# Attention scores over a ring of key tiles: one wide product per head in place of four narrow ones, and a 128-row low operand

## The chip, the cores and the metric

The kernel runs on one core of a Trainium2 chip. The core has five engines that run on their own and meet at semaphores: PE (matrix products; a product has a stationary operand that a separate load, PEld, brings in, and a moving operand that streams past it), DVE (vector), ACT (scalar functions), POOL, and SP, which here only issues transfers. The metric is the device time of one execution in microseconds (us). The kernel before takes 3162.19 us, the median of 3 runs from 3161.32 to 3166.99.

## The reference, cut to what matters

The program computes two blocks of a network on a sequence of 2048 positions. The change touches one part of the second block, an attention over a band of keys with 4 heads of width 64:

```python
q = rms_norm(q, q_g); k = rms_norm(k, k_g)
# a chunk of 64 queries sees its own chunk of keys and the 8 chunks before it
s = jnp.einsum('bqhd,bkhd->bhqk', qb, kb, preferred_element_type=jnp.float32) * scale + bias
p = jax.nn.softmax(s, axis=-1)
out = jnp.einsum('bhqk,bkhd->bqhd', p, vb)
```

Beside it the block has a linear recurrence over chunks (the names m_...), a convolution branch (c_...), two gates (the dense products called oz below) and an output product (fo).

## The kernel before, in words

The sequence is cut into 16 tiles of 128 positions. `cores` runs a loop over i = 0 to 15. Pass i finishes the attention of tile i (softmax weights turned by transposes, `a_turn`, tile pt; the product with the values, `a_pv`, tile pv) and already makes the scores of tile i+1: `a_own(i + 1)` the scores of the 4 heads against the tile's own 128 keys (tile s5 in the listings, s in the trace), `a_old(i + 1, h)` those of head h against up to four older key tiles (tile s4, also s in the trace). Tile 1 has one older tile, tile 2 two, tile 3 three, tiles 4 to 15 four.

Keys are held as two float16 numbers, a high and a low part. `kring` is a ring of 8 key tiles: partitions 0 to 63 hold the high part of the 64 key dimensions, partitions 64 to 127 the low part, then ring place, head, 128 keys. The query operand `qa` has the high part of q twice, in partitions 0 to 63 and 64 to 127, so that one product gives q-high times k-high plus q-high times k-low. The operand `ql` has the low part of q in 64 partitions, and meets the high part of the keys alone. A head's scores against one key tile are thus two products of 128 columns that add up in PSUM, one of 128 rows and one of 64 (`scored`, lines 1557 to 1562).

The order on every engine is the order of the calls in the loop, written out by hand. Between the attention and recurrence steps, `fill` puts in parts of a queue of dense products: one part is 3 products of 512 columns (oz, line 1465; from pass 14 on also fo, line 1839). `weave` puts in small DVE steps. All steps take their PSUM from four banks "b"; a bank is given out again when its last reader in program order is done. From pass 14 on each `fill` also carries one step that prepares the output weights (wo, lines 1825 and 1826: one ACT and one DVE instruction), from a tile wf that `stage` loads.

On DVE, `lowest` (line 1579) takes scores and bias and leaves the negative sum and its row minimum; on ACT, `a_soft` (line 1599) takes the exponential. For the turned weights ACT writes the high part (line 1616) and DVE the low part (line 1618, shown in the trace as line 41, tile p). After the loop, `finish` runs the rest of the output product.

Of the kernel before, what the change touches and what calls it, by code (L numbers as in the profile page):

```python
# [11 lines left out]
F16 = mybir.dt.float16  # L12
# [20 lines left out]
class Kernel:  # L33
# [1326 lines left out]
    def cores(self):  # L1360
        nc, a = self.nc, self.a
        A, B = self.pool("d2a"), self.pool("d2b", side="right")
# [4 lines left out]
        kring = self.slot(2, [128, 8, 4, 128], F16, "kring")  # L1367
# [11 lines left out]
        W = self.weights  # L1379
        st = {}  # L1380
        v1s = [B.tile([128, 4, 129], F32, name=f"v1_{j}") for j in range(2)]
        for t in v1s:
            nc.gpsimd.memset(t[:, :, 128:129], 1.0)
        tok = lambda i: slice(128 * i, 128 * i + 128)

        def load_a(i):

            if i > 15:
                return
            d = st.setdefault(i, {})  # L1390
            d["qa"] = A.tile([128, 4, 128], F16, name="qa", bufs=2)
            d["ql"] = A.tile([64, 4, 128], F16, name="ql", bufs=2)
            q, k = (x.rearrange("a (h p) t -> a p h t", p=64)[:, :, :, tok(i)] for x in (self.q_s, self.k_s))
            for j in range(2):
                nc.sync.dma_start(out=kring[64 * j:64 * j + 64, i % 8], in_=k[j])
                nc.sync.dma_start(out=d["qa"][64 * j:64 * j + 64], in_=q[0])
            nc.sync.dma_start(out=d["ql"], in_=q[1])
            nc.sync.dma_start(out=vring[:, i % 8], in_=self.av_s[tok(i)])

        def load_m(i):  # L1400
# [153 lines left out]

        first = lambda i: max(4 - i, 0)

        def scored(ps, i, h, j):

            d = st[i]
            r = kring[:, (i - 4 + j) % 8, h]  # L1560
            nc.tensor.matmul(out=ps, lhsT=d["qa"][:, h], rhs=r, start=True, stop=False)  # L1561
            nc.tensor.matmul(out=ps, lhsT=d["ql"][:, h], rhs=r[0:64], start=False, stop=True)  # L1562

        def a_own(i):
            if i > 15:
                return
            d = st[i]
            ps = self.bank("b", 4, name="s5")
            for h in range(4):
                scored(ps[:, 128 * h:128 * h + 128], i, h, 4)  # L1570
            d["mx"] = mx = A.tile([128, 8], F32, name="mx")
            d["sum"] = A.tile([128, 4], F32, name="sum", bufs=2)
            for h in range(4):
                lowest(s_[:, h, 512:], ps[:, 128 * h:128 * h + 128], bias[:, h, 512:], 3e38, mx[:, 4 + h:5 + h])
                weave()

        def lowest(out, x, y, start, least):

            nc.vector.tensor_tensor_reduce(out=out, in0=x, in1=y, scale=-1.0, scalar=start, op0=ALU.add, op1=ALU.min,
                                           accum_out=least)  # L1580

        def a_old(i, h):
            if i > 15:
                return
            lo = 128 * first(i)
            mx = st[i]["mx"]
            if i:
                ps = self.bank("b", 4, name="s4")
                for j in range(first(i), 4):
                    scored(ps[:, 128 * j:128 * j + 128], i, h, j)  # L1590
                lowest(s_[:, h, lo:512], ps[:, lo:512], bias[:, h, lo:512], mx[:, 4 + h:5 + h], mx[:, h:h + 1])

        def a_soft(i, h):
# [92 lines left out]
        def turn(i, j):  # L1686
# [14 lines left out]
            return lambda: self.sub(lo[:, c, s], h4(ps), hi[:, c, s])  # L1701

        load_a(0)
        load_m(0)
        load_rows(0, 0)
# [4 lines left out]
        load_z(0, 0)  # L1710
        load_u(0)
        load_a(1)
        lnp = B.tile([128, 2, 256], F32, name="lnp")
        nc.sync.dma_start(out=lnp, in_=a["lnp"])
# [11 lines left out]
        for i in range(16):  # L1726
# [11 lines left out]
            fill()  # L1738
            load_rows(i + 1, 0)
            load_a(i + 2)  # L1740
            fill()
            weave(2)
# [10 lines left out]
            low[0]()  # L1753
            weave()
            a_old(i + 1, 0)
            weave()
            fill()
# [5 lines left out]
            a_soft(i + 1, 0)  # L1763
            weave(2)
            a_old(i + 1, 1)
            low[2] = a_turn(i, 2)
            fill()
            weave(16)
            gate_mix(i - 1)
            a_pv(i, 1)  # L1770
            low[2]()
            a_old(i + 1, 2)
            fill()
            a_soft(i + 1, 1)
# [817 lines left out]
```

## Time and profile before

| | |
|---|---|
| median of 3 runs | 3162.19 us |
| the profiled execution's own time | 3160.66 us |
| its span, first to last instruction | 3158.9 us |
| PE busy | 3081.4 us, 98% |
| DVE busy | 2248.0 us, 71% |
| ACT busy | 1296.6 us, 41% |
| POOL busy | 265.2 us, 8% |
| score products (lines 1561 and 1562) | 280 and 280, from 2588.6 to 2961.7 us |

The span is that of one execution which the hardware profiler recorded; 1.8 us of its time lie outside it. The ends of matrix products are modelled in the record, so that PE durations overlap: what a product costs in a stream is read from the distance between starts, not from its duration. The loop over the 16 tiles takes the time from about 2590 to about 3000 us.

### The profile page before, as it was taken

The numbers are of one execution on the slowest core, as the hardware profiler recorded it, in microseconds if no ns is written. First come the engines' busy times: TensorE is split into PE (matmuls) and PEld (weight loads), VectorE is DVE, ScalarE is ACT, GpSimd is POOL, SyncE is SP. The second block draws the span as 40 slices with busy tenths as digits, with TensorE's granted clock in tenths as the row PEclk, the third lists the DMA queues.
The fourth block names the chain that finished last, engine by engine and source line by source line (L and its number), as shares of the span: only waits on it lengthen the run. The fifth ranks groups of instructions, "written<-read, shape, count | busy, mean of one in ns | idle before, by whom it ended". The sixth has DMA issues, their size and how long they took to land. (4 is left out here: it accounts for less than half of the span.)

```text
span 3158.9 us, 45408 instructions
## 1 busy us (share of the span) xinstructions
PE 3081.4 (98%) x16756; PEld 1589.5 (50%) x16756; DVE 2248.0 (71%) x4709; ACT 1296.6 (41%) x2796; POOL 265.2 (8%) x226
## 2 busy tenths in 40 slices
PE   7889998999999999999999999999999999999999
PEld 6664443444444444444444444645544446666644
DVE  8995668768887778777776656665677856776842
ACT  8983434544443335343443343311212225555610
POOL 0003444000000020000000333100000000000000
PEclk9999999999999999999999999999999999999999
DMA  4137776424442264343224310231121333323242
GB/s 158 53 104 266 271 268 213 137 84 122 125 123 82 82 226 132 110 132 106 80 80 133 121 40 16 94 125 59 51 77 68 107 115 91 84 85 88 76 157 83
DMA packets 295870, 365.30 MB, mean 116 GB/s; under 512 B 45088, under 2 KB 215008, under 8 KB 291424
## 3 DMA queue, kind: packets, MB, share of 16 engines
q1 hardware_dynamic: 291040, 354.02, 35.0%
q10 hardware_dynamic: 4608, 8.39, 0.7%
q8 instruction: 131, 2.15, 0.3%
q14 instruction: 91, 0.75, 0.1%
HBM read 257.98 MB, written 104.33 MB: 115 GB/s over the span
## 5 line engine op out<-in xcount | busy, mean ns | idle before, releaser
L267 PEld LDWEIGHTS <-w 128*128 128x128 f16 x4032 | 394.9, 98 | 480.9 <-issue 15.6
L735 PE MATMUL up<-y,w 128*128 128x512 f16 x2688 | 583.1, 379 | 0.0
L792 PE MATMUL dn<-x,w 128*128 128x512 f16 x1764 | 433.9, 380 | 7.6 <-DVE ss L59 3.8
L792 PEld LDWEIGHTS <-w 128*128 128x128 f16 x2688 | 263.7, 98 | 335.7 <-issue 21.3
L735 PEld LDWEIGHTS <-w 128*128 128x128 f16 x2688 | 263.0, 98 | 316.7
L267 PE MATMUL ga<-y,w 128*128 128x512 f16 x1536 | 335.0, 380 | 8.2 <-ACT sg L377 8.2
L792 PE MATMUL dn<-y,w 128*128 128x512 f16 x924 | 251.1, 381 | 6.5 <-DVE ss L59 3.1
L59 DVE SCALAR_TENSOR_TENSOR x<-dn,x 128x512 f32<-128x512 f32 x320 | 217.6, 688 | 51.0 <-PE dn L792 47.2
L1465 PE MATMUL oz<-oz,h 128*128 128x512 f16 x768 | 190.0, 386 | 0.0
L267 PE MATMUL pg<-h,w 128*128 128x512 f16 x768 | 171.4, 379 | 2.5 <-DVE h L41 2.5
L41 DVE TENSOR_TENSOR y<-up,y 128x512 f32<-128x512 f32 x128 | 88.4, 691 | 117.9 <-PE up L735 116.5
L1839 PE MATMUL fo<-mx,wo 128*128 128x512 f16 x768 | 167.4, 379 | 0.0
L267 PE MATMUL wide<-w,h 128*128 128x512 f16 x768 | 166.9, 379 | 0.0
L267 PE MATMUL mqk<-h,w 128*128 128x512 f16 x768 | 165.9, 379 | 0.0
L41 POOL TENSOR_TENSOR ss<-ss,sq 128x512 f32<-128x512 f32 x70 | 97.7, 1400 | 804.8 <-ACT sq L295 804.8
L267 PEld LDWEIGHTS <-h 128*128 128x128 f16 x1152 | 112.3, 98 | 99.5 <-DVE gif L59 4.0
L59 DVE SCALAR_TENSOR_TENSOR w<-ws,w 128x512 f16<-128x512 f32 x196 | 147.5, 758 | 17.2 <-ACT w L2430 15.9
L59 DVE SCALAR_TENSOR_TENSOR acc<-u,par,acc 128x512 f32<-128x512 f32 x232 | 159.2, 746 | 0.0
L2484 ACT ACTIVATE w<-sw 128x512 f16<-128x512 f32 x128 | 79.9, 625 | 150.4 <-DVE sw L41 150.0
L295 ACT ACTIVATE sq<-x 128x512 f32<-128x512 f32 x84 | 51.8, 628 | 177.3 <-DVE x L41 142.7
L1839 PEld LDWEIGHTS <-wo 128*128 128x128 f16 x768 | 75.0, 98 | 88.6
L1465 PEld LDWEIGHTS <-h 128*128 128x128 f16 x768 | 71.4, 99 | 68.4 <-issue 3.8
(403 smaller groups left out, 4596.2 us busy)
## 6 DMA issues: line engine op xcount, KB each, us to landing
w<-wd_s SPq DMA_DIRECT2D x448, 128.0 KB
ws<-w SPq DMA_DIRECT2D x64, 512.0 KB
wd_s<-pw SPq DMA_DIRECT2D x112, 256.0 KB
ws<-wd SPq DMA_DIRECT2D x34, 512.0 KB
pw<-w SPq DMA_DIRECT2D x32, 512.0 KB
y<-hop_s SPq DMA_DIRECT2D x20, 512.0 KB
xu<-xu SPq DMA_DIRECT2D x8, 1024.0 KB
tm<-rz_scr SPq DMA_DIRECT2D x64, 128.0 KB
```

Of the source, the lines that this page charges most:

```text
L41: f = lambda: (eng or self.nc.vector).tensor_tensor(out=out, in0=in0, in1=in1, op=op)
L59: f = lambda: self.nc.vector.scalar_tensor_tensor(out=out, in0=in0, scalar=s, in1=in1, op0=op0, op1=op1)
L267: self.nc.tensor.matmul(out=ps, lhsT=wk[p], rhs=xk[q], start=(first and i == 0 and j == 0), stop=(last and i == n - 1 and j == 2))
L295: self.nc.scalar.activation(out=sq, in_=x, func=ACT.Square, **kw)
L735: nc.tensor.matmul(out=ps[name], lhsT=ops[o][:, p, 128 * k:128 * k + 128], rhs=self.operand(o, k, q), start=(first and k == 0 and p + q == 0),
L792: nc.tensor.matmul(out=ps[mp, name], lhsT=w[:, 128 * p:128 * p + 128], rhs=x[:, q], start=(opens and c == 0 and p + q == 0), stop=(c == 1 ...
L1465: nc.tensor.matmul(out=d["bank", g], lhsT=x[:, k, s], rhs=y[:, c], start=(k == 0 and j == 0), stop=(k == 7 and j == 2))
L1839: self.nc.tensor.matmul(out=self.begun[m, n], lhsT=w[:, x, c], rhs=y[:, k], start=(k == 0 and j == 0), stop=(k == KT - 1 and j == 2))
L2484: nc.scalar.activation(out=out[q - 1][:, 0], in_=src[q - 1], func=ACT.Copy, scale=scale)
```

## The change

`ql` becomes a pair of tiles that are made once, of 128 partitions, whose lower half (partitions 64 to 127) is set to zero on POOL at the start; the loads write the first 64 partitions as before. The product with `ql` now takes all 128 partitions of `kring`, the low part of the keys meeting zeros. `scored` takes a count of ring places, and `a_old` calls it once for a head where the older tiles lie next to each other in the ring, and twice where they run over its end (for tiles 9, 10 and 11). The moving operand of such a product has up to 4 runs of 128 keys, one for each ring place, and 512 columns in all.

```diff
+        qls = [A.tile([128, 4, 128], F16, name=f"ql_{j}") for j in range(2)]
+        for t in qls:
+            nc.gpsimd.memset(t[64:128], 0.0)
         for t in v1s:
             nc.gpsimd.memset(t[:, :, 128:129], 1.0)
...
-            d["ql"] = A.tile([64, 4, 128], F16, name="ql", bufs=2)
+            d["ql"] = qls[i % 2]
...
-            nc.sync.dma_start(out=d["ql"], in_=q[1])
+            nc.sync.dma_start(out=d["ql"][0:64], in_=q[1])
...
-        def scored(ps, i, h, j):
+        def scored(ps, i, h, j, count=1):
 
             d = st[i]
-            r = kring[:, (i - 4 + j) % 8, h]
+            at = (i - 4 + j) % 8
+            r = kring[:, at:at + count, h]
+            ps = ps.rearrange("p (n c) -> p n c", n=count)
             nc.tensor.matmul(out=ps, lhsT=d["qa"][:, h], rhs=r, start=True, stop=False)
-            nc.tensor.matmul(out=ps, lhsT=d["ql"][:, h], rhs=r[0:64], start=False, stop=True)
+            nc.tensor.matmul(out=ps, lhsT=d["ql"][:, h], rhs=r, start=False, stop=True)
...
                 ps = self.bank("b", 4, name="s4")
-                for j in range(first(i), 4):
-                    scored(ps[:, 128 * j:128 * j + 128], i, h, j)
+                j = first(i)
+                while j < 4:
+                    count = min(4 - j, 8 - (i - 4 + j) % 8)
+                    scored(ps[:, 128 * j:128 * (j + count)], i, h, j, count)
+                    j += count
```

On PE, in a pass whose older tiles do not run over the ring's end, the place between `a_own` (s5) and head 0 of `a_old` (s4) had these rows before; the numbers behind the names tell one tile from another, and the size is partitions by columns of the result.

```order
L1561 LDWEIGHTS qa_21546
L1561 MATMUL s5_21893<-kring_20909,qa_21546 128x128
L1562 LDWEIGHTS ql_21547
L1562 MATMUL s5_21893<-kring_20909,ql_21547 128x128
L1561 LDWEIGHTS qa_21546
L1561 MATMUL s4_21914<-kring_20909,qa_21546 128x128
L1562 LDWEIGHTS ql_21547
L1562 MATMUL s4_21914<-kring_20909,ql_21547 128x128
```

Behind them stood three more groups like the last four rows, for the other three key tiles, and then the dense products. The same place after the change:

```order
L1567 LDWEIGHTS qa_21538
L1567 MATMUL s5_21867<-kring_20909,qa_21538 128x128
L1568 LDWEIGHTS ql_0_20915
L1568 MATMUL s5_21867<-kring_20909,ql_0_20915 128x128
L1567 LDWEIGHTS qa_21538
L1567 MATMUL s4_21888<-kring_20909,qa_21538 128x512
L1568 LDWEIGHTS ql_0_20915
L1568 MATMUL s4_21888<-kring_20909,ql_0_20915 128x512
L1469 LDWEIGHTS h1_15953
```

The head's 8 products are 2, of 512 columns; the own scores are as many as before; the dense products follow at once. Over the whole program 560 score products become 272. No other row of PE moves against its neighbours.

On POOL, ahead of the attention loop, the two new settings stand in front of the two old ones (v). Names in brackets are what the row waits for: queues of transfers (DMAHW) and engines.

```order
 L1195 COPY raw<-raw 128x3 [waits DVE_49,Activation_49,Pool_49] x2
-L1383 MEMSET v_0_20913 128x4 [waits DMAHW4_49,DMAHW3_49,DMAHW5_49,DMAHW2_49,DMAHW6_49,DMAHW1_49,DMAHW7_49,DMAHW0_49,PE_49]
-L1383 MEMSET v_1_20914 128x4
+L1385 MEMSET ql_20915 64x512 [waits DMAHW3_49,DMAHW2_49,DMAHW4_49,DMAHW1_49,DMAHW5_49,DMAHW0_49,DMAHW6_49,PE_49,DMAHW7_49,Activation_49,Pool_49]
+L1385 MEMSET ql_20916 64x512
+L1387 MEMSET v_0_20913 128x4 [waits Pool_49]
+L1387 MEMSET v_1_20914 128x4
```

They wait for the last transfers out of the memory that the attention's tiles take over; the old settings now stand behind them. SP's transfers keep their order, and DVE and ACT have the same rows as before.

## Rows read from the trace of the kernel before

**Rows 1.** The page: busy time by engine; granted clock in 40 slices, in tenths.

```profile
PE 3081.4 (98%) x16756; PEld 1589.5 (50%) x16756; DVE 2248.0 (71%) x4709; ACT 1296.6 (41%) x2796; POOL 265.2 (8%) x226
...
PEclk9999999999999999999999999999999999999999
```

**Rows 2.** Busy time by stretch: stretch, its length, engines, then granted clock, DMA.

```profile
2600.00:2610.00 10.00, 10.00 (x34) 4.05 (x34) 2.61 (x14) 3.32 (x14) 0.00 (x0) 0.50 0.81 224
...
2739.13:2764.99 25.86, 25.86 (x217) 17.63 (x216) 18.19 (x63) 14.37 (x45) 0.00 (x0) 1.00 0.30 86
```

**Rows 3.** Groups by line and shape, 2615 to 2980 us: count, busy us, mean ns.

```profile
L1561 PE MATMUL s<-kring,qa 128*128 128x128 f16 x268 | 61.0, 228 | 0.0
L1562 PE MATMUL s<-kring,ql 64*128 64x128 f16 x268 | 60.8, 227 | 0.0
```

**Rows 4.** PE in order of time, pass 6: start, duration, instruction, count.

```profile
2738.97 1.05 PE L1501 MATMUL ms<-qm,km 128*128 128x128 f32 x8
...
2743.32 1.04 PE L1614 MATMUL pt<-cst,s 128*128 128x128 f32 x8
2744.20 0.22 PE L1561 MATMUL s<-kring,qa 128*128 128x128 f16 x1
...
2746.76 2.12 PE L1465 MATMUL oz<-oz,h 128*128 128x512 f16 x9
2748.71 0.60 PE L1630 MATMUL pv<-vring,p 128*128 128x64 f16 x15
2749.14 0.22 PE L1561 MATMUL s<-kring,qa 128*128 128x128 f16 x1
...
2756.30 0.39 PE L1520 MATMUL num<-v,w 128*128 128x129 f32 x2
...
2764.83 1.05 PE L1501 MATMUL ms<-qm,km 128*128 128x128 f32 x8
```

**Rows 5.** PE's loads of stationary operands in the same pass, in order of time.

```profile
2743.32 0.80 PEld L1614 LDWEIGHTS pt<-cst,s 128*128 128x128 f32 x7
2744.09 0.10 PEld L1561 LDWEIGHTS <-qa 128*128 128x128 f16 x1
2744.34 0.09 PEld L1562 LDWEIGHTS <-ql 64*128 64x128 f16 x1 [0.16 <-issue]
```

**Rows 6.** DVE in the same pass; in brackets the idle time before, and its releaser.

```profile
2745.58 0.29 DVE L1579 CUSTOM_DVE_ANT_0 s<-s,bias 128x128 f32<-128x128 f32 x1 [1.12 <-PE s L1562]
...
2746.72 0.69 DVE L41 TENSOR_TENSOR p<-pt,p 128x512 f16<-128x512 f32 x1
...
2750.53 0.75 DVE L1579 CUSTOM_DVE_ANT_0 s<-s,bias,mx 128x512 f32<-128x512 f32 x1 [1.50 <-PE s L1562]
...
2753.11 0.68 DVE L41 TENSOR_TENSOR p<-pt,p 128x512 f16<-128x512 f32 x1
...
2758.49 0.16 DVE L41 TENSOR_TENSOR dn<-dn,gps 128x4 f32<-128x4 f32 x1 [1.25 <-ACT dn L1525]
```

**Rows 7.** The start of the loop: PE (two rows), SP's queue, and an earlier POOL setting.

```profile
2588.65 0.22 PE L1561 MATMUL s<-kring,qa 128*128 128x128 f16 x1 [2.03 <-DMA ql<-q_s]
...
2599.70 1.63 PE L1610 MATMUL pt<-cst,s 128*128 128x128 f32 x4 [2.27 <-ACT s L1599]
...
2584.32 0.61 SPq L1396 DMA_DIRECT2D qa<-q_s  x1
...
0.73 0.84 POOL L1916 MEMSET zero<- 128x896 f32 x1 [0.29 <-POOLq L2584]
```

**Rows 8.** Pass 14 in order of time: PE, DVE and ACT.

```profile
2957.76 0.60 PE L1630 MATMUL pv<-vring,p 128*128 128x64 f16 x15
...
2970.38 1.05 PE L1501 MATMUL ms<-qm,km 128*128 128x128 f32 x8
...
2956.39 0.68 DVE L41 TENSOR_TENSOR p<-pt,p 128x512 f16<-128x512 f32 x1
...
2955.09 0.98 ACT L1825 ACTIVATE wo<-wf,mlg 128x128 f16<-128x128 f32 x3 [3.20 <-DMA wf<-wout]
```

## The prediction, made before the changed kernel had run

> **What bounds the kernel now.** I read the page first, for the engine that bounds, then the attention loop by stretches, then one of its passes engine by engine, and last the two ends of the loop, where a pass is not like the others.
>
> PE is busy 98% of the span at a granted clock near full in every slice, DVE 71% [rows 1]. One whole pass, 2739.13 to 2764.99, shows PE busy for all of its 25.86 us at clock 1.00, DVE for 18.19 and ACT for 14.37 [rows 2]. So in the loop time is what PE takes, as long as DVE and ACT hand over in time. The reader should now see what PE pays for a score product. Between the starts at 2744.20 and 2746.76 [rows 4] stand 16 of them, four own pairs and head 0's four pairs: 2.56 us, 160 ns each, though each streams only 128 columns. In the same rows 9 dense products of 512 columns take 1.95 us, 216.7 ns each, and 15 value products of 64 columns 0.43 us, 28.7 ns each. These two kinds, all of 128 rows and each with a stationary operand of its own, lie on a line of 0.42 ns a column and about 2 ns a product. It gives 55.6 ns at 128 columns, 109 at 256, 163 at 384. A score product costs 104 ns more than the line.
>
> Where the 104 ns go is seen in PE's loads [rows 5]. The load of `qa` behind 128-row work starts at 2744.09, 0.11 us ahead of its product. The load of `ql`, the first of 64 rows, starts at 2744.34, only after PE waited 0.16 us for nothing that the trace shows. I read this as a load that cannot go ahead while the number of rows changes, at every product of a pair, since all alternate 128 and 64 rows.
>
> **The change part by part.** *Own scores, 8 products a pass.* Same columns, now all of 128 rows. Bounds: 160 ns (the padding does nothing) and 28.7 ns (the shortest step of 128-row float16 products). I take the line's 55.6, since both its ends are 128-row float16 products with a load each: 8 x 0.104 = 0.83 us saved.
>
> *Older scores, 4 heads a pass.* For four older tiles 8 x 160 ns = 1.28 us become 2 x 216.7 = 0.43: 0.85 a head, 3.39 a pass. For three tiles 0.635 a head, for two 0.42, for one 0.21. The moving operand has four runs of 128 where the dense one is a single run; I see no row for that, and take it as equal. Bounds are 216.7 ns and, if each run cost like a separate product, 4 x 55.6 = 222 ns, which is nothing to the sum. Over the ring's end (tiles 9 to 11) four products carry the same columns; at 2 ns each that is below 0.1 us in all.
>
> Sum on PE: a full pass saves 0.83 + 3.39 = 4.22 us; 12 passes (3 to 14) make 50.6. Passes 0, 1 and 2, with one, two and three older tiles, save 0.83 + 0.83, 0.83 + 1.69 and 0.83 + 2.54: 7.5. The own scores of tile 0, ahead of the loop, save 0.83. Together 59.0 us. The groups of this line confirm the scale: 268 of 280 pairs keep PE busy for 121.8 us by the modelled ends [rows 3], and 560 steps of 160 ns are 89.6.
>
> *What of it is not on the path.* Tile 0's 0.83 is lost: PE waits there for its load until 2588.65 and at 2599.70 once more, for ACT's exponential [rows 7], whatever it did between.
>
> *Whether DVE hands over in time* in a full pass. PE comes 0.83 earlier to the end of the own scores; DVE, which waited 1.12 us for them at 2745.58, can use 0.73 of it, since the last product's result comes late by its own length. Its low part of head 0's turned weights, 2746.72 to 2747.41 [rows 6], then ends at 2746.68. PE needs it in the value product of 2748.71, which comes 0.83 + 0.85 earlier, at 2747.03: 0.35 us to spare, where there were 1.3. DVE's next wait for PE, 1.50 at 2750.53, goes too: it gets there at about 2748.3, 2.26 earlier. The low part of head 2 (2753.11, 0.68 long) then ends at 2751.53. Its bank is the one that the recurrence product num takes, at 2756.30 - 4.22 = 2752.08: 0.55 to spare. From dn at 2758.49 on, DVE follows ACT and PE and all three move by 4.2. The pass is then 21.64 long, of which DVE is busy 18.19, 84%. So no wait takes the place of PE's work, but the spare is only a third to half a microsecond. Each full pass could lose up to some 1 us if handing over is slower than the rows say; I take 0.
>
> *Pass 14* is different: ACT waits until 2955.09 for the transfer wf, then prepares weights, and DVE's low part of head 1 stands behind its own share of that, 2956.39 to 2957.07 [rows 8]. This does not hang on the scores. The value product of head 1, at 2957.76, would come 2.52 earlier, at 2955.24, and so waits some 1.8 us for it. From there DVE, not PE, leads the pass, and it moves up only where it waited. Bounds of the loss in this pass: 1.8 and the whole 4.2. I take 2.5, nearer to the lower, since the dense products behind it still cover a part. Pass 15 has no scores and starts as much earlier as pass 14 ended (2970.38 [rows 8]).
>
> *The zeros.* Two settings of 64 x 512 float16 on POOL; one of 128 x 896 took 0.84 us [rows 7], so up to 0.5 each, estimated by elements in a row. They wait for the old memory, as the load of `qa` does, which started at 2584.32. They end near 2585.5, 3 us before the first score product. Covered; if not, the first product slips by that much, below 1 us. Loads keep their order and size; a pass that is 4 us shorter still leaves about a pass between a load and its use.
>
> Sum: 59.0 - 0.8 - 2.5 - 0.1 = 55.6, say 55.5. The span goes from 3158.9 to 3103.4, the execution's own time from 3160.66 to 3105.2. The median of the runs shown lies 1.5 above the profiled one, so I say 3106.7.
>
> **The rivals.** *The padding does nothing; only the wide products gain.* Then 104 ns are the cost of a load that no product covers, and stay on each product. The Trainium skill (TensorE: Matmul & The Clock Gate, Part 3, The mechanism) says that a load overlaps a running product only when their row groups differ; by that rule products that all have 128 rows would hide less, not more. A four-tile head would cost 2 x (160 + 384 x 0.42) = 0.64 us instead of 1.28. Over the passes this is 33 us, less 2.6 for the 24 extra products at the ring's end, 107 ns each: 30 saved, 3132. Against it speak the value products, 28.7 ns apart with a new operand each [rows 4], and the early load of `qa` behind 128-row work [rows 5]. By these rows the rule as it stands does not hold here.
>
> A smaller point of the same page (Part 2, Back-to-back issue gap) gives about 81 ns for a stream of products of 128 columns with loads. By that the own scores would save 3.2 us less, as an estimate; the page gives 131 ns at 512 columns, where this trace has 216.7, so I keep to the line.
>
> *DVE becomes the bound.* DVE's chain from the own scores to the low part of head 2 decides, if each of its hand-overs costs 0.5 us more than I read. Then 11 full passes lose 0.5 to 1.5 us each, 5 to 16: 3112 to 3123. For it: DVE at 84% and the thin spare above. Against it: its waits in the pass, 1.12, 1.50 and 1.25, are all for PE or for what PE releases.
>
> *Slower.* If PE had to wait for DVE about 2 us at a stretch in each pass, the clock could fall: behind the wait of 2.03 us at 2588.65 [rows 7] PE ran at 0.50, 1.2 of 2.4 GHz, from 2600 to 2610 [rows 2]. Half a pass at half clock costs some 11 us, so 12 passes would cost 130 and eat the gain; it decides from about 5 us a pass. I find no wait of that length in the timetable, pass 14's 1.8 being the longest.
>
> *No change* would need DVE or ACT to hold the pass at 25.86 already; they are busy 18.19 and 14.37 of it.
>
> **How the numbers follow.** Forecast, losses within about 4 us of mine, 0.70: 3101.5 to 3111. DVE as the bound 0.15, the padding without effect 0.10, slower 0.03, no change 0.02. The range takes in the forecast's bounds (no loss in any pass but the start: 3103.2 with median; a line that is a little steeper or flatter by 1%) and most of the DVE case: 3101 to 3119, leaving out about 0.15. A measurement of this kernel can tell about 0.2%, 6 us, from no change; faster by more than that is all of the first three cases, 0.95.
>
> **What would show it.** Right: own score products about 56 ns apart, older ones about 217 ns; loads of `ql` ahead of their products; passes of 21.6 us with PE still busy throughout; DVE's waits for s near zero; a PE wait for p of 1 to 2 us in pass 14. Wrong: score products still about 160 ns or more apart (first rival); PE waits for p or s in every pass (second); a clock of 0.50 inside the loop (third).

## The result, and the profile after

The changed kernel takes 3107.95 us, the median of 4 runs from 3104.74 to 3110.01, beside 3161.76 for the kernel before in the same session. The ratio is 0.982, with a 95% interval from 0.9804 to 0.9837: 1.8% faster. It was timed twice more beside later experiments, at 0.9817 and 0.982. The profiled execution took 3109.14 us, its span is 3107.3 us.

On the page PE is still the bound, with 56.4 us less of busy time than in [rows 1], and DVE has as much work as before:

```profile
PE 3025.0 (97%) x16468; PEld 1562.1 (50%) x16468; DVE 2248.2 (72%) x4709; ACT 1295.9 (42%) x2796; POOL 266.4 (9%) x228
...
PEclk9999999999999999999999999999999999999999
```

PE in order of time in pass 6 (start, duration, instruction, count) at the place that [rows 4] shows of before:

```profile
2723.98 0.22 PE L1567 MATMUL s<-kring,qa 128*128 128x128 f16 x1
2724.04 0.22 PE L1568 MATMUL s<-kring,ql 128*128 128x128 f16 x1
...
2724.43 0.38 PE L1567 MATMUL s<-kring,qa 128*128 128x512 f16 x1
2724.65 0.38 PE L1568 MATMUL s<-kring,ql 128*128 128x512 f16 x1
2724.86 2.11 PE L1469 MATMUL oz<-oz,h 128*128 128x512 f16 x9
2726.80 0.60 PE L1639 MATMUL pv<-vring,p 128*128 128x64 f16 x15
...
2731.79 0.39 PE L1524 MATMUL num<-v,w 128*128 128x129 f32 x2
```

Eight own products take the 0.45 us from 2723.98 to 2724.43, 56 ns each, where they took 160. A wide product takes 0.22 us (2724.43 to 2724.65, and from there to the dense products at 2724.86), so its four runs of 128 keys cost what one run of 512 does. PE's loads in the same place now start 0.05 to 0.1 us ahead of their products, as only the first `qa` did in [rows 5]; the gap of 0.16 us is gone:

```profile
2723.88 0.10 PEld L1567 LDWEIGHTS <-qa 128*128 128x128 f16 x1
2723.98 0.10 PEld L1568 LDWEIGHTS <-ql 128*128 128x128 f16 x1
2724.04 0.10 PEld L1567 LDWEIGHTS <-qa 128*128 128x128 f16 x1
```

The busy times of the pass (stretch, length, PE, PEld, DVE, ACT, POOL, granted clock, DMA share, GB/s), to be read beside [rows 2], show it 21.56 us long, with PE busy throughout. So it is over passes 1 to 13 together, from 2616.44 to 2891.34: PE is busy for 274.81 of the 274.90 us, at clock 1.00.

```profile
2718.76:2740.32 21.56, 21.56 (x191) 15.28 (x190) 17.96 (x63) 14.34 (x46) 0.00 (x0) 1.00 0.38 103
```

DVE in order of time, beside [rows 6]; the bracket is the idle time before and its releaser:

```profile
2724.63 0.29 DVE L1585 CUSTOM_DVE_ANT_0 s<-s,bias 128x128 f32<-128x128 f32 x1 [0.39 <-PE s L1568]
...
2725.78 0.68 DVE L41 TENSOR_TENSOR p<-pt,p 128x512 f16<-128x512 f32 x1
...
2726.45 0.74 DVE L1585 CUSTOM_DVE_ANT_0 s<-s,bias,mx 128x512 f32<-128x512 f32 x1
...
2730.57 0.68 DVE L41 TENSOR_TENSOR p<-pt,p 128x512 f16<-128x512 f32 x1
```

Its wait for the own scores fell from 1.12 to 0.39 us. The low part of head 0 ends at 2726.46, 0.34 before the first value product at 2726.80. The low part of head 2 ends at 2731.25, 0.54 before num at 2731.79.

Where the time came from, by the starts of the passes (PE's row of line 1505, 1501 before). Two later profiles of the changed kernel stand beside the first:

| us | before | after | after, 2nd | after, 3rd |
|---|---|---|---|---|
| pass 0 starts | 2591.66 | 2592.21 | 2594.32 | 2591.93 |
| passes 0 to 2 | 70.52 | 62.64 | 62.31 | 62.84 |
| passes 3 to 13 | 283.64 | 236.49 | 236.48 | 236.49 |
| pass 14 | 24.56 | 27.40 | 22.90 | 24.83 |
| pass 15 to the end | 188.5 | 188.6 | 187.8 | 188.5 |
| span | 3158.9 | 3107.3 | 3103.8 | 3104.6 |

The eleven full passes save 47.15 us, 4.29 each, to a few hundredths the same in every profile. Pass 14 lost time in the first profile, and differs by 4.5 us between three profiles of one kernel.

In the first profile that pass shows (PE, then DVE, then ACT, in order of time):

```profile
2900.92 0.31 PE L1639 MATMUL pv<-vring,p 128*128 128x64 f16 x5
2905.14 0.71 PE L1639 MATMUL pv<-vring,p 128*128 128x64 f16 x10 [3.91 <-DVE p L41]
2905.67 0.62 PE L1567 MATMUL s<-kring,qa 128*128 128x512 f16 x1
2906.07 0.64 PE L1568 MATMUL s<-kring,ql 128*128 128x512 f16 x1
...
2904.40 0.68 DVE L41 TENSOR_TENSOR p<-pt,p 128x512 f16<-128x512 f32 x1
...
2903.10 0.99 ACT L1834 ACTIVATE wo<-wf,mlg 128x128 f16<-128x128 f32 x3 [5.70 <-DMA wf<-wout]
```

ACT waits 5.70 us for the transfer wf; DVE's low part of head 1 stands behind its share of that weight preparation; PE waits 3.91 us for it. The wait stands ahead of a head's sixth value product, since the first five (`a_pv`) take no low part of the older weights. Behind the wait the wide products start 0.40 us apart instead of 0.22: the clock has fallen to half, as the busy times of the next 5 us show (the last three figures are the granted clock, DMA share and GB/s):

```profile
2905.00:2910.00 5.00, 4.86 (x23) 2.67 (x24) 4.91 (x15) 3.26 (x8) 0.00 (x0) 0.50 0.00 0
```

### The profile page after: what moved, and what is told of

It reads as the page before. It is cut to its first block, busy times and chain, and to the rows that moved or that the text cites. A ratio compares the mean times of both kernels' runs of the same rounds, so it can differ in the third digit from the quotient of the medians.

```text
span 3107.3 us, 44838 instructions
## 1 busy us (share of the span) xinstructions
PE 3025.0 (97%) x16468; PEld 1562.1 (50%) x16468; DVE 2248.2 (72%) x4709; ACT 1295.9 (42%) x2796; POOL 266.4 (9%) x228
```

## The experiments

My theory: 104 ns are the price of a change between 64 and 128 rows, paid at each change, and PE sets the length of a full pass as long as DVE has some third of a microsecond to spare at head 0. Rivals: the price belongs to each narrow product with a load, so only the wide products gain; or DVE is already the bound.

**Padding alone.** The changed kernel with the older scores again as single products of 128 columns, all of 128 rows.

```diff
-                j = first(i)
-                while j < 4:
-                    count = min(4 - j, 8 - (i - 4 + j) % 8)
-                    scored(ps[:, 128 * j:128 * (j + count)], i, h, j, count)
-                    j += count
+                for j in range(first(i), 4):
+                    scored(ps[:, 128 * j:128 * j + 128], i, h, j)
```

> The changed kernel with narrow products: the low operand has 128 rows (the lower 64 zeros), but the older scores keep one pair of products for each key tile, 128 columns each. My theory (the 104 ns are the price of a change between 128 and 64 rows): score products 56 ns apart, a four-tile head 0.44 us where wide products take 0.43, a pass near 21.7 us, and a time within 4 us of the changed kernel's, 3104 to 3112. Rival (a load that no product covers, padding without effect): 160 ns stay, a time near 3162.

Measured: 3107.09 us, ratio 0.9821 (0.9804 to 0.9837), so the padding alone gives the gain; the rival's 3162 is out. PE in order of time shows the 16 products of the own scores and head 0 in 0.89 us, and the pass is 0.07 us longer than with the wide ones:

```profile
2704.23 0.22 PE L1567 MATMUL s<-kring,qa 128*128 128x128 f16 x1
2704.28 0.22 PE L1568 MATMUL s<-kring,ql 128*128 128x128 f16 x1
...
2705.12 2.10 PE L1469 MATMUL oz<-oz,h 128*128 128x512 f16 x9
```

Its pass by busy times:

```profile
2720.63:2742.26 21.63, 21.63 (x215) 16.25 (x214) 18.03 (x63) 14.34 (x46) 0.00 (x0) 1.00 0.38 102
```

So 24 products fewer in a pass are worth some 3 ns each, and the change's more visible half, the wide products, adds next to nothing to the padding.

**Wide products alone.** The changed kernel with a `ql` of 64 partitions and no zeros.

```diff
-        qls = [A.tile([128, 4, 128], F16, name=f"ql_{j}") for j in range(2)]
-        for t in qls:
-            nc.gpsimd.memset(t[64:128], 0.0)
+        qls = [A.tile([64, 4, 128], F16, name=f"ql_{j}") for j in range(2)]
...
-            nc.tensor.matmul(out=ps, lhsT=d["ql"][:, h], rhs=r, start=False, stop=True)
+            nc.tensor.matmul(out=ps, lhsT=d["ql"][:, h], rhs=r[0:64], start=False, stop=True)
```

> The changed kernel with the low operand of 64 rows as before, and the wide products kept. My theory: each product still pays 104 ns for the change of rows, a four-tile head 2 x (217 + 104) = 0.64 us, own scores 160 ns apart, a pass near 23.3 us, a time of 3128 to 3136. Rival (the wide products do most of it, padding nothing of its own): a four-tile head 0.43 us, only the own scores stay at 160 ns, a pass near 22.5 us, 3114 to 3122.

Measured: 3135.09 us, ratio 0.991 (0.9895 to 0.9925): without the padding the wide products are worth 28.8 us, half of what the padding gives by itself. PE in order of time:

```profile
2712.54 0.22 PE L1565 MATMUL s<-kring,qa 128*128 128x128 f16 x1
2712.69 0.23 PE L1566 MATMUL s<-kring,ql 64*128 64x128 f16 x1
2712.85 0.23 PE L1565 MATMUL s<-kring,qa 128*128 128x128 f16 x1
...
2713.81 0.39 PE L1565 MATMUL s<-kring,qa 128*128 128x512 f16 x1
2714.13 0.39 PE L1566 MATMUL s<-kring,ql 64*128 64x512 f16 x1
2714.45 2.12 PE L1467 MATMUL oz<-oz,h 128*128 128x512 f16 x9
```

Narrow ones stay 0.16 us apart; a wide one takes 0.32, which is 0.217 and again 0.104. The price is the same at both widths: it does not go by columns. A head now has two changes of rows where it had eight, 24 fewer in a full pass, which is 2.58 us shorter than before. Busy times of a full pass, and of one whose older tiles run over the ring's end:

```profile
2707.31:2730.59 23.28, 23.28 (x191) 15.35 (x190) 18.20 (x63) 14.39 (x46) 0.00 (x0) 1.00 0.33 94
...
2777.16:2801.30 24.14, 24.14 (x199) 16.13 (x198) 18.18 (x63) 14.35 (x46) 0.00 (x0) 1.00 0.32 92
```

The second has 8 products more and is 0.86 us longer, 107 ns each. With 128 rows the passes over the ring's end are longer by 0.04 us at most.

**Grouping.** The kernel before, with 64 rows and narrow products, all of a bank's `qa` products first and then all its `ql` products: as many products and loads, but two changes of rows for a bank of 8 products where there were eight.

```diff
-                for j in range(first(i), 4):
-                    scored(ps[:, 128 * j:128 * j + 128], i, h, j)
+                for part in range(2):
+                    for j in range(first(i), 4):
+                        scored(ps[:, 128 * j:128 * j + 128], i, h, j, part, j == first(i), j == 3)
```

(`a_own` likewise; `scored` issues the one product that `part` names. The last two arguments mark the first product of a bank as the start of its sums and the last as their end, where before each pair had such marks of its own. Padding alone kept the marks of each pair and lost the price all the same, so the price isn't theirs.)

> The kernel before with the score products of a bank put in another order: first the four of 128 rows, then the four of 64 rows; sizes and count as before (560 products). My theory (the price is paid at a change of rows): two changes for eight products where there were eight, 8 x 0.056 + 2 x 0.104 = 0.65 us for a four-tile head or the own scores instead of 1.28, a pass near 22.7 us, a time of 3116 to 3126. Rival (a 64-row product, or its load, is slow by itself, 264 ns beside 56): no change, 3162.

Measured: 3123.79 us, ratio 0.9879 (0.9864 to 0.9893). PE in order of time:

```profile
2731.79 0.39 PE L1562 MATMUL s<-kring,qa 128*128 128x128 f16 x4
2732.11 0.39 PE L1564 MATMUL s<-kring,ql 64*128 64x128 f16 x4
2732.43 0.40 PE L1562 MATMUL s<-kring,qa 128*128 128x128 f16 x4
```

PE's loads for the four products at 2732.11:

```profile
2732.11 0.22 PEld L1564 LDWEIGHTS <-ql 64*128 64x128 f16 x4
```

Four products take 0.32 us: four steps of 55.6 ns and one price of about 100. The first load behind the change starts no earlier than its product, at 2732.11; the loads behind it go on without such a gap. Its pass is 22.72 us long:

```profile
2726.56:2749.28 22.72, 22.72 (x216) 16.29 (x215) 18.21 (x63) 14.39 (x46) 0.00 (x0) 1.00 0.33 97
```

That is 3.14 us less than before for 30 changes fewer in five banks, 105 ns each. Neither the products nor the loads became fewer or wider, and no zeros were added: the price sits at the change of rows. A 64-row product is not slow by itself, and the rival's 3162 is out here too.

**DVE's spare, in both kernels.** Three additions of 128x128 on a tile that nobody reads, once a pass, on DVE behind the own scores.

```diff
+        idle = A.tile([128, 128], F32, name="idle")
+        nc.vector.memset(idle, 0.0)
...
             a_own(i + 1)
+            for _ in range(3):
+                self.add(idle, idle, idle)
             low[0]()
```

In the kernel before:

> The kernel before with three more DVE additions of 128 x 128 in each pass, which nobody reads, ahead of the low part of head 0's turned weights, some 0.6 to 0.9 us together. Both theories: no PE wait, no change of the time beyond the noise, since that low part had 1.3 us to spare. It is the comparison for the same additions in the changed kernel.

Measured: 3164.31 us, ratio 1.0001 (0.9992 to 1.001). A full pass is as long as before, 25.86 us, with PE busy throughout and DVE 0.78 us busier:

```profile
2718.88:2744.74 25.86, 25.86 (x216) 17.62 (x214) 18.97 (x66) 14.36 (x46) 0.00 (x0) 1.00 0.30 85
```

In the changed kernel, beside that kernel itself:

> The changed kernel once more, as the comparison for the two runs beside it: 3104 to 3111. In pass 14 PE waits for the low part of head 1's turned weights behind the transfer wf; how long hangs on when wf lands, 1.8 us if it takes the 4.7 us of the kernel before, 3.9 if it takes 7.2 as in the first profile.

> The changed kernel with the same three additions on DVE as in the comparison on the kernel before, 0.6 to 0.9 us a pass. My theory (the low part of head 0 has 0.35 us to spare): PE waits for it 0.2 to 0.6 us in each full pass, 3 to 7 us more than the changed kernel beside it. Rival (DVE is already the bound of the pass): the whole 0.6 to 0.9 in each pass, 8 to 11 us. Second rival (ample spare): no change.

Measured: 3106.43 us for the changed kernel, and 3113.54 us, ratio 0.9842 (0.9829 to 0.9855), with the additions; the spans differ by 6.0. DVE, PE and the pass of the kernel with them:

```profile
2728.93 0.94 DVE L41 TENSOR_TENSOR idle<-idle 128x128 f32<-128x128 f32 x3
2729.78 0.68 DVE L41 TENSOR_TENSOR p<-pt,p 128x512 f16<-128x512 f32 x1
...
2730.52 0.47 PE L1639 MATMUL pv<-vring,p 128*128 128x64 f16 x10 [0.26 <-DVE p L41]
```

```profile
2721.90:2743.94 22.04, 21.78 (x191) 15.24 (x190) 18.74 (x66) 14.10 (x46) 0.00 (x0) 1.00 0.35 100
```

The medians differ by 7.1 us, at the upper end of the 3 to 7 expected. The additions hold DVE for 0.85 us (2728.93 to 2729.78), and the pass grows by 0.47 of them. (The row's 0.26 is counted from the modelled end of the product before, so it is shorter than what the wait costs.) The rest, 0.38, was the spare; the prediction had worked out 0.35. So the changed kernel isn't bound by DVE, but it is 0.4 us away from it, while the one before took in the same 0.85 us a pass with no change of its length.

**Pass 14: the preparing steps later.** The changed kernel with five empty entries ahead of the weight preparation, so that its first step comes five fills later.

```diff
+        if j == 0:
+            self.prep += [lambda: None] * 5
```

> The changed kernel with the preparation of the output weights begun five dense parts later in pass 14, so that ACT and DVE do their attention steps before they wait for wf. My theory (wf's landing stops ACT, then DVE, then PE, and the idle PE loses its clock): no wait of PE for p in pass 14 above 1 us, clock 1.00, the pass 20 to 22 us instead of 27.4, and 3 to 7 us less than the changed kernel beside it. Rival (DVE is the bound of passes 14 and 15 anyway, and the wait only shows it): the gain comes back as waits in pass 15, less than 2 us in all.

Measured: 3105.45 us, ratio 0.9811 (0.9798 to 0.9825). Pass 14 is 20.67 us long at clock 1.00, and the wait for p is gone. But in pass 15 PE waits for the weights themselves:

```profile
2893.94:2914.61 20.67, 20.62 (x186) 14.65 (x184) 17.81 (x64) 13.92 (x44) 0.00 (x0) 1.00 0.43 135
...
2917.32 0.39 PE L1850 MATMUL fo<-mx,wo 128*128 128x512 f16 x1 [1.22 <-ACT wo L1834]
2918.00 1.90 PE L1850 MATMUL fo<-mx,wo 128*128 128x512 f16 x8 [0.29 <-DVE wo L59]
```

Against the second profile of the changed kernel pass 14 gains 2.2 us, and the stretch behind it loses 1.3 (189.1 against 187.8). The median is 1.0 us lower, less than these runs can tell. So pass 14 did what I expected, but the gain of 3 to 7 us did not come: as the rival had it, it went back into waits of pass 15 and left less than 2 us. These waits are for the preparing steps on ACT and DVE, which now come too late for their products.

**Pass 14: half of the transfer first.** The changed kernel once more, and the changed kernel with the first transfer of wf cut into two of 512 KB, the columns that are needed first in front.

```diff
-        nc.sync.dma_start(out=f, in_=self.a["wout"][j])
+        if j == 0:
+            for c in range(2):
+                nc.sync.dma_start(out=f[:, 1024 * c:1024 * c + 1024], in_=self.a["wout"][j][:, 1024 * c:1024 * c + 1024])
+        else:
+            nc.sync.dma_start(out=f, in_=self.a["wout"][j])
```

> The changed kernel a third time, beside the next one. Full passes 21.57 us, as in both profiles so far. Pass 14 was 27.40 us where the first half megabyte and more of wf, one transfer of 1024 KB, came 7.2 us after its issue, and 22.90 where it came after 4.7. If the arrival of that transfer sets the length of pass 14, this profile lies on the same line: about 20.3 us, plus 2.5 us at 4.7 us of transfer, and some 1.8 us more for each further us. If pass 14 is long for a reason of its own, it doesn't follow the transfer. Median near 3106.5 us.

> The changed kernel with the first transfer of wf cut in two, 512 KB each, the columns of the first eight preparing steps first. Theory (PE waits in pass 14 for DVE, DVE for ACT's first preparing step, that for wf): the first half arrives some 2 to 3 us earlier, so PE's wait for p in pass 14 (1.40 and 3.91 us in the two profiles of the changed kernel) is below 0.3, the pass 20.4 to 21.2 us long, at a clock of 1.00 throughout, and pass 15 follows without the wait for wo of 1.2 us that the later steps brought. Worth 1.5 to 6 us of span by the profiles, so a median of 3101 to 3106. Rival (the transfer is not it, DVE's added load in pass 14 is): pass 14 stays at 22.9 us or more.

Measured: 3106.89 us (ratio 0.982, 0.9806 to 0.9834) and 3106.02 us (0.9815, 0.98 to 0.983): no difference. The cut transfer's rows of SP's queue, ACT and PE:

```profile
2901.01 0.82 SPq L1829 DMA_DIRECT2D wf<-wout  x2
...
2905.68 0.98 ACT L1838 ACTIVATE wo<-wf,mlg 128x128 f16<-128x128 f32 x3 [3.15 <-DMA wf<-wout]
...
2907.72 0.47 PE L1639 MATMUL pv<-vring,p 128*128 128x64 f16 x10 [1.37 <-DVE p L41]
```

The half came 4.67 us after its issue, no earlier than the whole did in the quickest case (4.70); that I had wrong, and the wait stayed. With the other profiles it still gives a line. The time is from the issue of wf to ACT's first preparing step; the clock is the lowest that was granted in stretches of 5 us from 2900 to 2920:

| kernel | wf | PE's wait for p | pass 14 | clock |
|---|---|---|---|---|
| first half ahead | 4.67 | 1.37 | 22.85 | 1.00 |
| changed, 2nd | 4.70 | 1.40 | 22.90 | 1.00 |
| changed, 3rd | 5.79 | 2.49 | 24.83 | 0.77 |
| padding alone | 6.23 | 2.91 | 25.29 | 0.78 |
| changed, 1st | 7.21 | 3.91 | 27.40 | 0.50 |

In the three profiles of the one kernel the wait grows by 1.09 where the transfer grows by 1.09, and by 1.42 where it grows by 1.42. The third profile lies on the line that its expectation drew: 24.8 us of pass 14 for a landing after 5.79, 24.83 measured. DVE's load in the pass is the same in all three (19.1 to 19.3 us busy), so it can't make the difference; the arrival of wf does. The pass grows by 1.8 times as much, since behind the longer waits PE runs at a lower clock: of the 4.50 us between the second profile and the first, 2.10 are more idle time of PE in the pass and 2.40 more busy time, at a mean granted clock of 0.88 instead of 1.00.

## Why the prediction was right, point by point

**The price of a score product** was right in size and place. 104 ns was read from the distance between starts and from loads that came late; three readings of two other runs give it again: 105 ns for each change of rows (grouping), and with wide products alone 107 for each extra product at the ring's end and 0.104 us at 512 columns. The Trainium skill (TensorEngine Tiling (Array Packing), Tiling Modes, Key Properties) says that a change of the tiling mode drains TensorE. It names no price; the grouped run, with its 105 ns for each change, agrees with it, though no row here shows a drain as such.

**The line** held, at 56 ns and 0.22 us: full passes save 4.29 where the sum had 4.22. Passes 0 to 2 saved 7.7 to 8.2, where it had 7.5.

**The first rival** fell with padding alone: the price goes although no product got wider. Its 3132 is near the 3135.09 measured with wide products alone, where the price does stay on each product, but because the rows still change. The rule that it drew on (the Trainium skill, TensorE: Matmul & The Clock Gate, Part 3, The mechanism: a load overlaps running products only where row groups differ) does not hold here as that sentence stands: loads of 128 rows, 0.10 us long, follow one another every 56 ns, and their products do too.

**DVE as the bound** fell: PE shows no wait in passes 1 to 13. The spare was sized nearly rightly, 0.38 us in the run against 0.35, with some luck in it. The prediction took the first value product as the one that needs the low part. The sixth does, some 0.14 later, and where PE waited for it (2730.52 behind the end of p at 2730.46) handing over took 0.06, which the prediction left out; the two make up for each other in part. The second spare, at head 2, was forecast at 0.55 and is 0.54. DVE's wait for s is 0.39, not near zero as I wrote under what would show it; the working itself (0.73 used of 1.12) leaves 0.39.

**Pass 14** is the term that was mis-sized. The chain was right (wf, ACT, DVE's low part, PE), and the second profile loses 4.29 - (24.56 - 22.90) = 2.6 us, as forecast. But the first loses 4.29 + 2.84 = 7.1 and the third 4.6, outside the bounds of 1.8 to 4.2; and of the three waits for p, 1.40, 2.49 and 3.91 us, only the first lies in the 1 to 2 that was forecast. The failed step is "this does not hang on the scores", with a bound that took the landing of wf from one profile as fixed: it varies from 4.7 to 7.2 us after the same issue, and a longer wait costs clock besides, which I had weighed for each full pass but not here. So the sign of the rival "slower", a low clock inside the loop, did come, in this one pass: 0.50 over 5 us in the first profile and 0.77 in the third.

**The zeros.** POOL and PE at the start of the loop, first profile of the changed kernel:

```profile
2584.98 1.01 POOL L1385 MEMSET ql<- 64x512 f16 x2 [10.75 <-DMA mlg<-mlg]
...
2589.08 0.22 PE L1567 MATMUL s<-kring,qa 128*128 128x128 f16 x1 [2.02 <-DMA ql<-q_s]
```

Both settings together take 1.01 us and end at 2586.0, half a microsecond later than estimated; the first score product waits for the load of `ql` until 2589.08, so they were covered. They did not hold up that load either: SP issues it 3.07 us behind the first load of `kring`, where it was 3.08 before.

**The total** came out 1.3 us from the forecast. That is nearer than runs of the one kernel lie to each other (3104.74 to 3110.01), so how near it came is in part luck. In the first profile the larger loss in pass 14 (4.6 us more than forecast) and a start 0.55 later were partly made up by passes 0 to 13 (1.1 us more saved than forecast); the profile's span of 3107.3 lies 3.9 above the 3103.4 worked out; the second's, 3103.8, lies 0.4 above. The landing of wf is on record only for the profiled executions, not for the others that the median is taken from, and the start of pass 0 moves by some microseconds between profiles too, from 2591.66 to 2596.99 in all those made here. What sets that start wasn't followed.

## What to carry to other kernels

Where products of 64 rows stand among products of 128, padding their operand with zeros to 128 rows can be worth more than fewer or wider products: here padding alone gave 57 us and wide products alone 29. It takes away 0.1 us at every change for the same columns, and mere grouping of those with as many rows already gave 40 us. When the bound engine gets faster, look for a pass in which another engine's queue stands behind a transfer: a wait that was covered comes out there, and its size needs the landing times of several profiles, not of one.

## What the runs showed of the hardware that was not expected

The same transfer of 1024 KB, issued at the same place of the pass, was followed by ACT's first preparing step between 4.70 and 7.21 us later, in four profiles of kernels that leave it whole. The DMA view of the 10 us around it (GB/s in 40 slices of a quarter microsecond), first profile of the changed kernel:

```profile
GB/s 338 289 248 258 201 137 285 217 199 215 150 213 82 66 164 229 426 360 360 360 426 459 426 131 229 66 33 33 33 33 33 33 33 33 0 0 0 0 0 0
```

and the second:

```profile
GB/s 238 336 340 285 266 287 189 147 66 16 262 0 66 262 197 328 492 524 426 426 360 360 492 0 0 0 0 0 0 0 0 0 0 0 0 0 0 0 0 0
```

In the second the transfer ends at some 430 GB/s; in the first it trails off at 33 GB/s for 2 us. The busy times of this tail (the last three figures are the granted clock, DMA share and GB/s):

```profile
2900.50:2902.50 2.00, 0.73 (x8) 0.37 (x6) 0.00 (x0) 0.00 (x0) 0.00 (x0) 1.00 0.08 33
```

A share of 0.08 of the 16 DMA engines is the work of little more than one. I read that as one engine finishing late; no view names the engine, and why it does is open.
